# One bank for both heads of a pair in the attention units with one or two blocks of keys, and eight low parts of the output weights on POOL

## The chip, the cores and the metric

The kernel runs on one core of a Trainium2 chip. The metric is the device time of one execution in microseconds (us). The engines are named as in the profile: PE is TensorE, with PEld its weight loads; DVE is VectorE, ACT ScalarE, POOL GpSimd, SP SyncE. SP issues most of the DMAs.

## The reference

Two layers; each is a feed-forward block, a token mixer and a second feed-forward block, each followed by a layer norm. The sequence has 512 positions, the model 1024 features. The change lies in the mixer, whose attention parts are these, per block of 128 queries:

```
def diff_attention_block(q_blk, start, k1, k2, v, lam):     # 4 heads, two softmaxes each
    def probs(qi, ki):
        sc = jnp.einsum('bhqd,bhkd->bhqk', qi, ki).astype(jnp.float32) * scale
        return jax.nn.softmax(jnp.where(causal, sc, -jnp.inf), axis=-1)
    w = probs(q1, k1) - lam * probs(q2, k2)
    return jnp.einsum('bhqk,bhkd->bhqd', w.astype(v.dtype), v)

def stick_breaking_block(q_blk, start, k, v):                # 4 heads
    z = jnp.einsum('bhqd,bhkd->bhqk', q_blk, k).astype(jnp.float32) * (B_HEAD_DIM ** -0.5)
    log_stay = jnp.where(strict, jax.nn.log_sigmoid(-z), 0.0)
    log_tail = lax.cumsum(log_stay, axis=3, reverse=True) - log_stay
    w = jnp.where(strict, jnp.exp(jax.nn.log_sigmoid(z) + log_tail), 0.0)
    return jnp.einsum('bhqk,bhkd->bhqd', w.astype(v.dtype), v)
```

The third part of the mixer is a gated delta rule over chunks, which needs the inverses of triangular matrices and then a scan over the sequence. The three outputs are normed, the third is gated, and the concatenation is multiplied with the output weights (1024 by 1024).

## The kernel before

All data are 32-bit and feature-major. A product with weights is three matmuls (L103 to L105): the activations and the weights are each split into a high part and a low part, and the product of the two low parts is left out. Weights come from HBM in chunks of 512 KB (L81) to a ring of two buffers. ACT casts each half of a chunk to the high part (L89); the low part is the difference (L90), on DVE or, where `st.eng` says so, on POOL. In the mixer, from the first projections on, `st.eng` is POOL, until `st.eng = st.queue = None` ahead of the output projection. Such a weight tile has 24 matmuls of 512 columns, called fills below where they go into time that other work leaves on PE.

The order of the instructions on each engine comes from a scheduler that goes by dependencies, buffers and the order in which the program emits its work, so a change in the emission moves rows on every engine. In the mixer the emission is this: query and key projections of the stick-breaking heads; values; `attend(1, 0)` and `attend(1, 1)` (stick-breaking, a pair of heads each); twelve convolved tiles; one projection of queries and keys for the differential heads; `triangles()`; `attend(0, 0)`, in which `between` emits the second such projection (its evictions are L510 on ACT and L511 on DVE); `delta()`; `attend(0, 1)`; `outputs()`; the four gate tiles; the output projection with its norm.

- `attend` works on a pair of heads in units, one for a block of 128 queries (qt 0 to 3) and one head: (qt 2, 3, 1, 0) by two heads, eight units. A unit of block qt has (qt + 1) blocks of keys. The `between` work is emitted after the fourth unit. Each unit's values are emitted one unit later (`later`).
- `unit` takes a score bank in PSUM for each score row (`psc`, two banks), L880 and L881. For the differential heads there are two score rows each: maximum (L917), exponential with its sum (L467), then a reciprocal (L922), a factor (L923) and the combination (L926). For stick-breaking heads: absolute value (L933), exponential and logarithm (L467 twice), L936, a scan from the back (L939), L940, an exponential (L467). The values are transposes to the bank `pt` (L904), a copy (L906) and the products to the bank `po` (L909).
- `triangles` ends in `base`: blocks of 16 by 16 go to the scratch in HBM (L675) and back in another layout (L692), are inverted on DVE in fifteen pairs of dependent operations (L700, L702), copied (L704), written out (L703, L705) and read back as `XT` and `X` (L708, L710). The names in the profile of what is read are `XT` and `inv`.
- `delta` doubles the inverted blocks: for each of four heads products L718, L723 and transposes L727, with an ACT copy or a DVE subtraction (L724) after each. `join` (L738 to L752) follows.
- `outputs` is the scan over the chunks (`scan`, L773 to L798), in which a product waits for DVE and DVE for a product; the norms of its results (`emit`).
- The output projection (`head`) first multiplies the first half of the contraction for four output tiles, which takes eight parts of weights (a part is half a chunk), then the other half, and adds each tile to the norm's sums (L157 to L168).

Of the kernel before, what the change touches and what calls it, by code (L numbers as in the profile page):

```python
# [9 lines left out]
F32 = mybir.dt.float32  # L10
# [416 lines left out]
def mixer(g, l):  # L427
# [446 lines left out]
    def scores(q, k, qt, i, which):  # L874

        n = (qt + 1) * P
        dgn = ch(qt)
        sc = py()
        for j, t in enumerate(k[i]):
            nc.tensor.matmul(out=sc[:, 0:n], lhsT=q[i][0][:, dgn], rhs=t[:, 0:n], start=j == 0, stop=False)  # L880
        nc.tensor.matmul(out=sc[:, dgn], lhsT=g.identb, rhs=g.maskb[:, which], start=False, stop=True)  # L881
        return sc

    def attend(which, j, between=None):
# [3 lines left out]
        units = [(qt, i) for qt in (2, 3, 1, 0) for i in range(2)]  # L888
        for n, (qt, i) in enumerate(units):
            nxt = unit(which, qt, 2 * j + i, po, su[:, qt, i], P * qt + 64 * i)  # L890
            while len(later) > 1:
                later.pop(0)()
            later.append(nxt)
            if between and n == 3:
                between()
        later.append(lambda: finish(which, j, po, su))

    def unit(which, qt, h, po, su, col):
        n = (qt + 1) * P

        def values(w):
            pt = pav.tile([P, T], F32, name="pt")
            for k in range(qt + 1):
                nc.tensor.transpose(out=pt[:, ch(k)], in_=w[:, ch(k)], identity=g.ident)  # L904
            wT = at.tile([P, T], F32, name="at")
            nc.scalar.copy(out=wT[:, 0:n], in_=pt[:, 0:n])  # L906
            vc = 256 * which + 64 * h
            for k in range(qt + 1):
                nc.tensor.matmul(out=po[:, col:col + 64], lhsT=wT[:, ch(k)], rhs=V[k][:, vc:vc + 64],  # L909
                                 start=k == 0, stop=k == qt)  # L910

        def diff():
            mx = sm.tile([P, 2], F32, name="mx")
            pr = []
            for i in range(2):
                sc = scores(qa, ka, qt, 2 * h + i, 0)
                nc.vector.tensor_reduce(out=mx[:, i:i + 1], in_=sc[:, 0:n], axis=mybir.AxisListType.X, op=ALU.max, negate=True)  # L917
                p = at.tile([P, T], F32, name="at")
                act(out=p[:, 0:n], in_=sc[:, 0:n], func=AF.Exp, bias=mx[:, i:i + 1], accum_out=su[:, i:i + 1])
                pr.append(p)  # L920
            cf = sm.tile([P, 2], F32, name="cf")
            nc.vector.reciprocal(out=cf[:, 0:1], in_=su[:, 1:2])  # L922
            nc.vector.scalar_tensor_tensor(out=cf[:, 1:2], in0=su[:, 0:1], scalar=g.nlam[:, l:l + 1], in1=cf[:, 0:1],  # L923
                                           op0=ALU.mult, op1=ALU.mult)
            p1, p2 = pr
            nc.vector.scalar_tensor_tensor(out=p1[:, 0:n], in0=p2[:, 0:n], scalar=cf[:, 1:2], in1=p1[:, 0:n],  # L926
                                           op0=ALU.mult, op1=ALU.add)
            return lambda: values(p1)

        def stick():  # L930
            sc = scores(qb, kb_, qt, h, 1)
            e = at.tile([P, T], F32, name="at")
            nc.scalar.activation(out=e[:, 0:n], in_=sc[:, 0:n], func=AF.Abs)  # L933
            act(out=e[:, 0:n], in_=e[:, 0:n], func=AF.Exp, scale=-1.0)
            act(out=e[:, 0:n], in_=e[:, 0:n], func=AF.Ln, bias=1.0)
            nc.vector.scalar_tensor_tensor(out=e[:, 0:n], in0=sc[:, 0:n], scalar=0.0, in1=e[:, 0:n], op0=ALU.max, op1=ALU.add)  # L936
            cs = e
            back = e[:, 0:n][:, ::-1]
            nc.vector.tensor_tensor_scan(out=cs[:, 0:n][:, ::-1], data0=back, data1=back, initial=0.0, op0=ALU.add, op1=ALU.bypass)  # L939
# [319 lines left out]
```

## Time and profile before

| | |
|---|---|
| median of three runs | 2250.42 us (2246.45 to 2251.85) |
| profiled execution, its own time | 2250.16 us |
| its span, first to last instruction | 2248.4 us |
| mean granted clock of TensorE in it | 0.985 of full |
| PE busy | 2138.2 us, 95% of the span |
| DVE, ACT, POOL busy | 1169.6, 907.9 and 377.5 us |

The profile is of one execution. Busy PE time is modelled for pipelined matmuls, so that one matmul's duration overlaps the next one's. The times of a row are from the start of the span. The first layer's mixer runs from about 400 to 760 us, the second layer's from about 1515 to 1875 us, with the same pattern.

### The profile page before, as it was taken

The numbers are of one execution on the slowest core, as the hardware profiler recorded it, in microseconds if no ns is written. First come the engines' busy times: TensorE is split into PE (matmuls) and PEld (weight loads), VectorE is DVE, ScalarE is ACT, GpSimd is POOL, SyncE is SP. The second block draws the span as 40 slices with busy tenths as digits, with TensorE's granted clock in tenths as the row PEclk, the third lists the DMA queues.
The fourth block names the chain that finished last, engine by engine and source line by source line (L and its number), as shares of the span: only waits on it lengthen the run. The fifth ranks groups of instructions, "written<-read, shape, count | busy, mean of one in ns | idle before, by whom it ended". The sixth has DMA issues, their size and how long they took to land. (4 is left out here: it accounts for less than half of the span.)

```text
span 2248.4 us, 30132 instructions
## 1 busy us (share of the span) xinstructions
PE 2138.2 (95%) x11382; PEld 1782.6 (79%) x11382; DVE 1169.6 (52%) x2363; ACT 907.9 (40%) x1801; POOL 377.5 (17%) x327
## 2 busy tenths in 40 slices
PE   8999999999798999999999999999987989999997
PEld 7888889777677888888888888897776768888886
DVE  4533436386578833343663334263774788333426
ACT  4333324575464533332443333245753535333313
POOL 1100011426204400000130000023461234000010
PEclk9999999999899999999999999999998999999998
DMA  6423323514512233332333333234144123333322
GB/s 190 125 94 95 98 75 104 139 40 122 129 58 72 84 109 94 94 94 75 116 109 95 94 94 94 66 104 131 57 133 109 48 85 94 95 96 100 95 66 94
DMA packets 90898, 217.32 MB, mean 97 GB/s; under 512 B 21968, under 2 KB 36336, under 8 KB 90752
## 3 DMA queue, kind: packets, MB, share of 16 engines
q1 hardware_dynamic: 82848, 187.47, 27.5%
q10 hardware_dynamic: 6912, 25.17, 3.8%
q0 software_dynamic: 992, 2.75, 0.7%
q8 instruction: 90, 1.47, 0.3%
q14 instruction: 56, 0.46, 0.1%
HBM read 193.83 MB, written 6.83 MB: 89 GB/s over the span
## 5 line engine op out<-in xcount | busy, mean ns | idle before, releaser
L89 ACT CAST whi<-wraw 128x512 fp32r<-128x512 f32 x692 | 421.4, 619 | 959.4 <-PE pd L104 755.1
L90 DVE TENSOR_TENSOR wlo<-wraw,whi 128x512 fp32r<-128x512 f32 x580 | 431.0, 751 | 658.6 <-ACT whi L89 647.4
L103 PE MATMUL pd<-x,whi 128*128 128x512 f32 (+1 forms) x1920 | 726.7, 380 | 12.9 <-ACT x L1177 6.2
L105 PE MATMUL pd<-x,wlo 128*128 128x512 f32 (+1 forms) x1920 | 728.3, 380 | 3.2 <-DVE wlo L90 3.2
L104 PE MATMUL pd<-x,whi 128*128 128x512 f32 (+1 forms) x1920 | 727.7, 379 | 1.6 <-POOL x L231 1.3
L103 PEld LDWEIGHTS pd<-x,whi 128*128 128x128 f32 x1920 | 365.8, 191 | 77.5 <-ACT x L1177 6.2
L105 PEld LDWEIGHTS pd<-x,wlo 128*128 128x128 f32 x1920 | 366.2, 191 | 67.4 <-DVE wlo L90 3.4
L104 PEld LDWEIGHTS pd<-x,whi 128*128 128x128 f32 x1920 | 366.2, 191 | 66.8 <-POOL x L231 3.0
L103 PE MATMUL pd<-hhi,whi 128*128 128x512 f32 (+1 forms) x880 | 307.7, 350 | 0.0
L104 PE MATMUL pd<-hlo,whi 128*128 128x512 f32 (+1 forms) x880 | 307.7, 350 | 0.0
L105 PE MATMUL pd<-hhi,wlo 128*128 128x512 f32 (+1 forms) x880 | 307.3, 349 | 0.0
L168 POOL TENSOR_TENSOR lt<-lt 128x512 f32<-128x512 f32 x26 | 38.9, 1497 | 1065.3 <-ACT lt L165 1065.3
L103 PEld LDWEIGHTS pd<-hhi,whi 128*128 128x128 f32 x880 | 165.5, 188 | 24.4
L105 PEld LDWEIGHTS pd<-hhi,wlo 128*128 128x128 f32 x880 | 165.4, 188 | 24.1
L104 PEld LDWEIGHTS pd<-hlo,whi 128*128 128x128 f32 x880 | 165.5, 188 | 24.1
L90 POOL TENSOR_TENSOR wlo<-wraw,whi 128x512 fp32r<-128x512 f32 x112 | 150.2, 1357 | 138.7 <-ACT whi L89 70.1
L259 DVE TENSOR_TENSOR lt<-pd,lt 128x512 f32<-128x512 f32 x88 | 60.4, 689 | 111.9 <-PE pd L105 110.7
L231 POOL TENSOR_TENSOR x<-x 128x256 fp32r<-128x256 f32 x60 | 45.1, 753 | 162.5 <-ACT x L229 132.7
L134 POOL TENSOR_TENSOR x<-x 128x512 f32<-128x512 f32 x48 | 70.9, 1522 | 0.0
L261 DVE TENSOR_TENSOR hlo<-lt,hhi 128x512 fp32r<-128x512 f32 x88 | 67.0, 765 | 6.3
L165 ACT ACTIVATE lt<-x 128x256 f32<-128x256 f32 (+1 forms) x58 | 29.7, 512 | 95.8 <-DVE x L163 95.5
L568 DVE SCALAR_TENSOR_TENSOR kqv<-pd,conv,kqv 128x511 f32<-128x511 f32 (+2 forms) x72 | 53.5, 743 | 20.1 <-ACT kqv L566 18.9
(309 smaller groups left out, 2287.9 us busy)
## 6 DMA issues: line engine op xcount, KB each, us to landing
wraw<-in_w SPq DMA_DIRECT2D x308, 512.0 KB, 3.5
wraw<-in_w ACTq DMA_DIRECT2D x48, 512.0 KB, 3.6
kqv<-kqv SPq DMA_DIRECT2D x128, 64.0 KB, 2.0
kqv<-kqv SPq DMA_DIRECT2D x48, 128.0 KB, 4.7
scr<-zero POOLq DMA_DIRECT2D x2, 1032.0 KB, 11.1
x<-in_xT SPq DMA_DIRECT2D x8, 256.0 KB, 5.5
scr<-inv SPq DMA_DIRECT2D x8, 256.0 KB, 2.7
XT<-scr SPq DMA_DIRECT2D x8, 256.0 KB, 4.8
```

Of the source, the lines that this page charges most:

```text
L89: nc.scalar.copy(out=hi, in_=r)
L90: (eng or self.eng or nc.vector).tensor_tensor(out=lo, in0=r, in1=hi.bitcast(F32), op=ALU.subtract)
L103: nc.tensor.matmul(out=out, lhsT=whi, rhs=xhi, start=first, stop=False)
L104: nc.tensor.matmul(out=out, lhsT=whi, rhs=xlo, start=False, stop=False)
L105: nc.tensor.matmul(out=out, lhsT=wlo, rhs=xhi, start=False, stop=last)
L134: i = g.nc.gpsimd.tensor_tensor(out=t, in0=xhi.bitcast(F32), in1=xlo.bitcast(F32), op=ALU.add)
L165: nc.scalar.activation(out=sq[:, r], in_=t[:, r], func=AF.Square)
L168: eng.tensor_tensor(out=self.acc2[:, r], in0=self.acc2[:, r], in1=sq[:, r], op=ALU.add)
L231: eng.tensor_tensor(out=xlo[:, r], in0=t[:, r], in1=xhi[:, r].bitcast(F32), op=ALU.subtract)
L259: nc.vector.tensor_tensor(out=sg, in0=pu, in1=sg, op=ALU.mult)
L261: nc.vector.tensor_tensor(out=hlo, in0=sg, in1=hhi.bitcast(F32), op=ALU.subtract)
L568: nc.vector.scalar_tensor_tensor(out=y[:, s:], in0=p[:, :T - s], scalar=wc[:, 3 - s:4 - s], in1=y[:, s:], op0=ALU.mult, op1=ALU.add)
```

## The change

A unit with one or two blocks of keys now takes both heads of the pair. The score rows of both heads stand side by side in one bank of 512 columns: for stick-breaking heads two rows of 256 or 128 columns, for differential heads two rows of 256 to a bank (two banks) or four rows of 128. Operations without a scalar of their own per row go over the whole bank: the maximum (now L928, with two or four results), the reciprocal and the factor (L936, L937), the stick-breaking chain except its scan, and the copy of the transposed weights. The exponentials of the differential heads, the scans and the combinations (now L941) stay one per row or head. `attend` so has six units for eight. The `between` work is emitted after the third unit. In the output projection `st.eng` stays POOL for the first half's eight parts of weights.

```diff
-    def scores(q, k, qt, i, which):
-
-        n = (qt + 1) * P
+    def scores(out, q, k, qt, i, which):
+
         dgn = ch(qt)
-        sc = py()
         for j, t in enumerate(k[i]):
-            nc.tensor.matmul(out=sc[:, 0:n], lhsT=q[i][0][:, dgn], rhs=t[:, 0:n], start=j == 0, stop=False)
-        nc.tensor.matmul(out=sc[:, dgn], lhsT=g.identb, rhs=g.maskb[:, which], start=False, stop=True)
-        return sc
+            nc.tensor.matmul(out=out, lhsT=q[i][0][:, dgn], rhs=t[:, 0:(qt + 1) * P], start=j == 0, stop=False)
...
-        units = [(qt, i) for qt in (2, 3, 1, 0) for i in range(2)]
-        for n, (qt, i) in enumerate(units):
-            nxt = unit(which, qt, 2 * j + i, po, su[:, qt, i], P * qt + 64 * i)
+        units = [(2, (0,)), (2, (1,)), (3, (0,)), (3, (1,)), (1, (0, 1)), (0, (0, 1))]
+        for n, (qt, hs) in enumerate(units):
+            nxt = unit(which, qt, j, hs, po, su)
             while len(later) > 1:
                 later.pop(0)()
             later.append(nxt)
-            if between and n == 3:
+            if between and n == 2:
                 between()
...
-    def unit(which, qt, h, po, su, col):
+    def unit(which, qt, j, hs, po, su):
         n = (qt + 1) * P
-
-        def values(w):
+        m = len(hs)
+        heads = [2 * j + i for i in hs]
+
+        def values(ws):
             pt = pav.tile([P, T], F32, name="pt")
-            for k in range(qt + 1):
-                nc.tensor.transpose(out=pt[:, ch(k)], in_=w[:, ch(k)], identity=g.ident)
+            for i, w in enumerate(ws):
+                for k in range(qt + 1):
+                    nc.tensor.transpose(out=pt[:, i * n + k * P:i * n + (k + 1) * P], in_=w[:, ch(k)], identity=g.ident)
             wT = at.tile([P, T], F32, name="at")
-            nc.scalar.copy(out=wT[:, 0:n], in_=pt[:, 0:n])
-            vc = 256 * which + 64 * h
-            for k in range(qt + 1):
-                nc.tensor.matmul(out=po[:, col:col + 64], lhsT=wT[:, ch(k)], rhs=V[k][:, vc:vc + 64],
-                                 start=k == 0, stop=k == qt)
+            nc.scalar.copy(out=wT[:, 0:m * n], in_=pt[:, 0:m * n])
+            for i, h in enumerate(heads):
+                vc = 256 * which + 64 * h
+                col = P * qt + 64 * hs[i]
+                for k in range(qt + 1):
+                    nc.tensor.matmul(out=po[:, col:col + 64], lhsT=wT[:, i * n + k * P:i * n + (k + 1) * P],
+                                     rhs=V[k][:, vc:vc + 64], start=k == 0, stop=k == qt)
...
+        def parts(x, c):
+            return [x[:, i * n:(i + 1) * n] for i in range(c)]
 
         def diff():
-            mx = sm.tile([P, 2], F32, name="mx")
+            mx = sm.tile([P, 4], F32, name="mx")
+            todo = [(h, i) for h in range(m) for i in range(2)]
+            per = T // n
             pr = []
-            for i in range(2):
-                sc = scores(qa, ka, qt, 2 * h + i, 0)
-                nc.vector.tensor_reduce(out=mx[:, i:i + 1], in_=sc[:, 0:n], axis=mybir.AxisListType.X, op=ALU.max, negate=True)
+            for a in range(0, 2 * m, per):
+                now = todo[a:a + per]
+                c = len(now)
+                sc = py()
+                for (h, i), o in zip(now, parts(sc, c)):
+                    scores(o, qa, ka, qt, 2 * heads[h] + i, 0)
+                nc.vector.tensor_reduce(out=mx[:, a:a + c], in_=sc[:, 0:c * n].rearrange("p (c t) -> p c t", t=n),
+                                        axis=mybir.AxisListType.X, op=ALU.max, negate=True)
                 p = at.tile([P, T], F32, name="at")
-                act(out=p[:, 0:n], in_=sc[:, 0:n], func=AF.Exp, bias=mx[:, i:i + 1], accum_out=su[:, i:i + 1])
-                pr.append(p)
-            cf = sm.tile([P, 2], F32, name="cf")
-            nc.vector.reciprocal(out=cf[:, 0:1], in_=su[:, 1:2])
-            nc.vector.scalar_tensor_tensor(out=cf[:, 1:2], in0=su[:, 0:1], scalar=g.nlam[:, l:l + 1], in1=cf[:, 0:1],
+                for b, ((h, i), o, y) in enumerate(zip(now, parts(sc, c), parts(p, c))):
+                    act(out=y, in_=o, func=AF.Exp, bias=mx[:, a + b:a + b + 1], accum_out=su[:, qt, hs[h], i:i + 1])
+                    pr.append(y)
+            cf = sm.tile([P, 2, 2], F32, name="cf")
+            sv = su[:, qt, hs[0]:hs[0] + m]
+            nc.vector.reciprocal(out=cf[:, 0:m, 0], in_=sv[:, :, 1])
+            nc.vector.scalar_tensor_tensor(out=cf[:, 0:m, 1], in0=sv[:, :, 0], scalar=g.nlam[:, l:l + 1], in1=cf[:, 0:m, 0],
...
-            p1, p2 = pr
-            nc.vector.scalar_tensor_tensor(out=p1[:, 0:n], in0=p2[:, 0:n], scalar=cf[:, 1:2], in1=p1[:, 0:n],
-                                           op0=ALU.mult, op1=ALU.add)
-            return lambda: values(p1)
+            for h in range(m):
+                p1, p2 = pr[2 * h:2 * h + 2]
+                nc.vector.scalar_tensor_tensor(out=p1, in0=p2, scalar=cf[:, h, 1:2], in1=p1, op0=ALU.mult, op1=ALU.add)
+            return lambda: values(pr[::2])
...
-            sc = scores(qb, kb_, qt, h, 1)
+            sc = py()
+            for h, o in zip(heads, parts(sc, m)):
+                scores(o, qb, kb_, qt, h, 1)
+            sc = sc[:, 0:m * n]
             e = at.tile([P, T], F32, name="at")
-            nc.scalar.activation(out=e[:, 0:n], in_=sc[:, 0:n], func=AF.Abs)
-            act(out=e[:, 0:n], in_=e[:, 0:n], func=AF.Exp, scale=-1.0)
-            act(out=e[:, 0:n], in_=e[:, 0:n], func=AF.Ln, bias=1.0)
-            nc.vector.scalar_tensor_tensor(out=e[:, 0:n], in0=sc[:, 0:n], scalar=0.0, in1=e[:, 0:n], op0=ALU.max, op1=ALU.add)
-            cs = e
-            back = e[:, 0:n][:, ::-1]
-            nc.vector.tensor_tensor_scan(out=cs[:, 0:n][:, ::-1], data0=back, data1=back, initial=0.0, op0=ALU.add, op1=ALU.bypass)
-            nc.vector.tensor_tensor(out=cs[:, 0:n], in0=sc[:, 0:n], in1=cs[:, 0:n], op=ALU.subtract)
-            act(out=cs[:, 0:n], in_=cs[:, 0:n], func=AF.Exp)
-            return lambda: values(cs)
+            cs = e[:, 0:m * n]
+            nc.scalar.activation(out=cs, in_=sc, func=AF.Abs)
+            act(out=cs, in_=cs, func=AF.Exp, scale=-1.0)
+            act(out=cs, in_=cs, func=AF.Ln, bias=1.0)
+            nc.vector.scalar_tensor_tensor(out=cs, in0=sc, scalar=0.0, in1=cs, op0=ALU.max, op1=ALU.add)
+            for y in parts(e, m):
+                back = y[:, ::-1]
+                nc.vector.tensor_tensor_scan(out=back, data0=back, data1=back, initial=0.0, op0=ALU.add, op1=ALU.bypass)
+            nc.vector.tensor_tensor(out=cs, in0=sc, in1=cs, op=ALU.subtract)
+            act(out=cs, in_=cs, func=AF.Exp)
+            return lambda: values(parts(e, m))
...
-    st.eng = st.queue = None
+    st.queue = None
...
             if b < KD:
                 for d in range(4):
                     st.get(bo + d * KD + PC)
+                st.eng = None
                 st.use([g.ws] * 3 + [g.wx] * 5)
```

The built program has the same PE instructions in another order. On ACT it has 48 fewer of about 1790 over both layers, on DVE 68 fewer, 16 of them low parts (L90), which POOL has more. The order of three places follows, as rows of line, operation, output from inputs and shape.

On DVE, the beginning of the fifteen pairs of `base` in the first layer, while `attend(0, 0)` runs, before:

```order
L700 TENSOR_TENSOR blkt<-blk 128x15
L926 SCALAR_TENSOR_TENSOR at<-at,cf 128x512
L702 TENSOR_TENSOR blk<-blk,blkt 128x15
L917 TENSOR_REDUCE mx<-psc 128x1
L700 TENSOR_TENSOR blkt<-blk 128x28
L922 RECIPROCAL cf<-su 128x1
L917 TENSOR_REDUCE mx<-psc 128x1
L702 TENSOR_TENSOR blk<-blk,blkt 128x14x2
L923 SCALAR_TENSOR_TENSOR cf<-su,nlam,cf 128x1
L700 TENSOR_TENSOR blkt<-blk 128x39
L926 SCALAR_TENSOR_TENSOR at<-at,cf 128x512
L702 TENSOR_TENSOR blk<-blk,blkt 128x13x3
```

and of the change:

```order
L700 TENSOR_TENSOR blkt<-blk 128x15
L928 TENSOR_REDUCE mx<-psc 128x1
L702 TENSOR_TENSOR blk<-blk,blkt 128x15
L928 TENSOR_REDUCE mx<-psc 128x2
L700 TENSOR_TENSOR blkt<-blk 128x28
...
L928 TENSOR_REDUCE mx<-psc 128x2
L700 TENSOR_TENSOR blkt<-blk 128x48
L702 TENSOR_TENSOR blk<-blk,blkt 128x12x4
L700 TENSOR_TENSOR blkt<-blk 128x55
L702 TENSOR_TENSOR blk<-blk,blkt 128x11x5
L928 TENSOR_REDUCE mx<-psc 128x4
L700 TENSOR_TENSOR blkt<-blk 128x60
```

Before, reductions of one score row stand between the pairs; the eight of the one- and two-block units reach to the eleventh pair. In the change the reductions of those units are three, the last ahead of the sixth pair; from the first L700 to L704 it is 46 rows, where it was 55. The L511 that follows L704 (the second projection's keys) keeps its place.

On PE, from the last unit of `attend(0, 0)` to the doubling of the first heads, before (L103 to L105 are gate fills, L718, L723 and L727 the doubling):

```order
L909 MATMUL po<-kqv,at 128x64 x2
L904 MATMUL pt<-ident,at 128x128
L103 MATMUL pd<-x,whi 128x512
L104 MATMUL pd<-x,whi 128x512
L105 MATMUL pd<-x,wlo 128x512
...
L718 MATMUL pa<-inv,lt 128x128 x4
L105 MATMUL pd<-x,wlo 128x512
...
L723 MATMUL pa<-XT,inv 128x128 x4
L105 MATMUL pd<-x,wlo 128x512
...
L727 MATMUL pa<-ident,XT 128x128 x4
L718 MATMUL pa<-inv,lt 128x128 x4
```

and of the change:

```order
L911 MATMUL po<-kqv,at 128x64 x4
L904 MATMUL pt<-ident,at 128x128 x4
L103 MATMUL pd<-x,whi 128x512
L104 MATMUL pd<-x,whi 128x512
L105 MATMUL pd<-x,wlo 128x512
...
L105 MATMUL pd<-x,wlo 128x512
L718 MATMUL pa<-inv,lt 128x128 x4
L723 MATMUL pa<-XT,inv 128x128 x4
L727 MATMUL pa<-ident,XT 128x128 x4
L718 MATMUL pa<-inv,lt 128x128 x4
L723 MATMUL pa<-XT,inv 128x128 x4
```

Before, eight of the second gate tile's fills stood between the last L904 and the first L718, and its other sixteen behind it, among the first two heads. In the change the first gate tile's 24 fills stand ahead of the last scores, all 24 of the second's between the last L904 and the first L718, and none among the heads' L718, L723 and L727. Within the scan of `outputs`, from its first L779 to its last L798, stand 52 weight matmuls, where 35 stood.

On POOL, from the end of `triangles` to the first norm's application in the first layer (L995, now L1013, is the split of the attention outputs, L134 the residual, L168 a norm sum), before:

```order
L715 TENSOR_TENSOR lt<-inv,mask 128x512 x2
L695 MEMSET blk 128x256
L696 MEMSET blk 128x16
L90 TENSOR_TENSOR wlo<-wraw,whi 128x512 x2
L995 TENSOR_TENSOR kqv<-x,kqv 128x256 x8
L134 TENSOR_TENSOR x<-x 128x512 x8
L168 TENSOR_TENSOR lt<-lt 128x512 x3
L90 TENSOR_TENSOR wlo<-wraw,whi 128x512 x8
L231 TENSOR_TENSOR x<-x 128x256 x12
```

and of the change:

```order
L715 TENSOR_TENSOR lt<-inv,mask 128x512 x2
L90 TENSOR_TENSOR wlo<-wraw,whi 128x512
L695 MEMSET blk 128x256
L696 MEMSET blk 128x16
L90 TENSOR_TENSOR wlo<-wraw,whi 128x512 x7
L1013 TENSOR_TENSOR kqv<-x,kqv 128x256 x8
L134 TENSOR_TENSOR x<-x 128x512 x8
L90 TENSOR_TENSOR wlo<-wraw,whi 128x512 x2
L168 TENSOR_TENSOR lt<-lt 128x512 x2
L90 TENSOR_TENSOR wlo<-wraw,whi 128x512
L168 TENSOR_TENSOR lt<-lt 128x512
L90 TENSOR_TENSOR wlo<-wraw,whi 128x512 x7
L231 TENSOR_TENSOR x<-x 128x256 x12
```

Six of the eight moved low parts stand ahead of the split of the attention outputs; two stand behind the residual, and the third norm sum stands behind one low part that is loaded ahead.

## Rows read from the trace of the kernel before

**Rows 1.** The page, busy time, share of the span and count of each engine.

```profile
PE 2138.2 (95%) x11382; PEld 1782.6 (79%) x11382; DVE 1169.6 (52%) x2363; ACT 907.9 (40%) x1801; POOL 377.5 (17%) x327
```

**Rows 2.** Stretches: length, busy us of PE, PEld, DVE, ACT, POOL, granted clock, DMA.

```profile
430.00:512.00 82.00, 77.63 (x412) 60.27 (x411) 62.63 (x122) 59.20 (x138) 28.02 (x21) 0.98 0.15 45
571.00:581.00 10.00, 7.82 (x27) 5.81 (x27) 7.61 (x19) 4.52 (x12) 4.58 (x6) 0.50 0.53 116
576.00:602.00 26.00, 19.74 (x103) 15.90 (x102) 15.02 (x62) 9.06 (x28) 2.55 (x2) 0.83 0.33 73
620.00:660.00 40.00, 40.00 (x402) 31.14 (x402) 28.42 (x83) 22.89 (x65) 0.00 (x0) 1.00 0.18 54
660.00:700.00 40.00, 34.40 (x209) 27.26 (x208) 29.84 (x112) 18.95 (x46) 15.96 (x16) 1.00 0.05 14
723.00:730.00 7.00, 1.44 (x9) 1.22 (x8) 6.93 (x14) 2.68 (x6) 4.05 (x4) 0.86 0.33 88
1690.00:1716.00 26.00, 18.31 (x105) 15.06 (x105) 15.15 (x62) 9.08 (x29) 2.55 (x2) 0.89 0.36 78
```

**Rows 3.** ACT by line and shape, 430 to 760: busy us, mean ns, idle before.

```profile
L467 ACT ACTIVATE at<-at 128x256 f32<-128x256 f32 x12 | 4.7, 411 | 0.2
L467 ACT ACTIVATE at<-at 128x128 f32<-128x128 f32 x12 | 3.7, 306 | 1.6 <-DVE at L940 1.6
```

**Rows 4.** DVE and POOL by line and shape in the same stretch.

```profile
L917 DVE TENSOR_REDUCE mx<-psc 128x1 f32<-128x512 f32 x8 | 5.4, 680 | 1.1 <-PE psc L881 1.1
L917 DVE TENSOR_REDUCE mx<-psc 128x1 f32<-128x256 f32 x8 | 3.3, 416 | 3.2 <-PE psc L881 3.2
L917 DVE TENSOR_REDUCE mx<-psc 128x1 f32<-128x128 f32 x8 | 2.3, 289 | 1.1 <-PE psc L881 1.0
L922 DVE RECIPROCAL cf<-su 128x1 f32<-128x1 f32 x16 | 2.5, 157 | 1.4 <-ACT at L467 1.4
L923 DVE SCALAR_TENSOR_TENSOR cf<-su,nlam,cf 128x1 f32<-128x1 f32 x16 | 4.5, 283 | 0.1
L90 DVE TENSOR_TENSOR wlo<-wraw,whi 128x512 fp32r<-128x512 f32 x19 | 14.3, 770 | 11.1 <-ACT whi L89 11.1
L90 POOL TENSOR_TENSOR wlo<-wraw,whi 128x512 fp32r<-128x512 f32 x43 | 58.5, 1376 | 56.7 <-ACT whi L89 24.2 <-ACT at L467 10.4 <-PE pd L104 7.0
```

**Rows 5.** DVE in order of time around base: start, us, work, wait before it.

```profile
578.40 0.18 DVE L702 TENSOR_TENSOR blk<-blk,blkt 128x15 f32<-128x15 f32 x1
580.96 0.42 DVE L917 TENSOR_REDUCE mx<-psc 128x1 f32<-128x256 f32 x1 [2.39 <-PE psc L881]
592.70 1.12 DVE L702 TENSOR_TENSOR blk<-blk,blkt 128x15 f32<-128x15 f32 x1
593.86 0.37 DVE L704 COPY blk<-blk 128x256 f32<-128x256 f32 x1
594.15 0.68 DVE L511 SCALAR_TENSOR_TENSOR kqv<-pd,kqv 128x512 fp32r<-128x512 f32 x1
```

**Rows 6.** POOL in order of time beside them.

```profile
592.53 1.26 POOL L90 TENSOR_TENSOR wlo<-wraw,whi 128x512 fp32r<-128x512 f32 x1 [5.23 <-ACT whi L89]
```

**Rows 7.** PE in order of time from base to the doubling.

```profile
594.89 0.79 PE L103 MATMUL pd<-x,whi 128*128 128x512 f32 x1 [2.35 <-DVE kqv L511]
595.48 0.63 PE L104 MATMUL pd<-x,whi 128*128 128x512 f32 x1
595.90 0.63 PE L105 MATMUL pd<-x,wlo 128*128 128x512 f32 x1
601.92 2.04 PE L718 MATMUL pa<-inv,lt 128*128 128x128 f32 x8 [3.36 <-DMA inv<-scr]
608.87 1.06 PE L718 MATMUL pa<-inv,lt 128*128 128x128 f32 x8
613.04 1.06 PE L718 MATMUL pa<-inv,lt 128*128 128x128 f32 x8
617.26 1.06 PE L718 MATMUL pa<-inv,lt 128*128 128x128 f32 x8
```

More of the change, by code (lines that the diff above doesn't have):

```diff
@@ L872, in mixer @@
     oab = [None] * 4
-    def scores(q, k, qt, i, which):
-        n = (qt + 1) * P
+    def scores(out, q, k, qt, i, which):
         dgn = ch(qt)
-        sc = py()
         for j, t in enumerate(k[i]):
-            nc.tensor.matmul(out=sc[:, 0:n], lhsT=q[i][0][:, dgn], rhs=t[:, 0:n], start=j == 0, stop=False)
-        nc.tensor.matmul(out=sc[:, dgn], lhsT=g.identb, rhs=g.maskb[:, which], start=False, stop=True)
-        return sc
+            nc.tensor.matmul(out=out, lhsT=q[i][0][:, dgn], rhs=t[:, 0:(qt + 1) * P], start=j == 0, stop=False)
+        nc.tensor.matmul(out=out[:, dgn], lhsT=g.identb, rhs=g.maskb[:, which], start=False, stop=True)
     def attend(which, j, between=None):
```

## The prediction

> **What bounds the kernel now.** I read the page's busy times first: PE is busy 95% of the span, the next engine 52% [rows 1]. So nothing is gained by less work on ACT or DVE as such, only where PE waits for them. The table of stretches then says where that is. In the stick-breaking stretch of 82 us PE works 77.63 and sits idle 4.37, with ACT busy 59.20 and DVE 62.63. Around `base` it works 19.74 of 26 us at a granted clock of 0.83; in the second layer's like stretch 18.31 of 26 at 0.89. For the ten us from 571 the clock is 0.50, its lower level of 1.2 GHz. From 620 to 660 PE has no idle time at all, from 660 to 700, in the scan, 5.60 us; and in the output projection it works 1.44 of the 7 us from 723, with DVE busy 6.93 [rows 2]. Last I read DVE and PE in order of time around `base`. There one chain sets the end: the fifteen pairs on DVE finish at L704 (593.86), the inverse goes to HBM and back, and the first product that uses it starts at 601.92, 8.06 us later, after PE has waited 3.36 [rows 5, 7]. Ahead of that PE waited 2.35 for an L511 that stands behind L704 on DVE, because its bank had to come free for a gate fill [rows 5, 7].
>
> **The change part by part.** All for one layer; the second is taken alike, by the two stretches above.
>
> *Stick-breaking units.* Of the sixteen units, eight become four. Each shared one drops three activations, an absolute value and a copy on ACT, and two operations on DVE. An activation of 256 columns takes 0.411 us and two of 128 take 0.612 [rows 3], so about 0.20 goes with each of 20 ACT operations: 4.0 us of 59.20. I price the eight dropped DVE operations like the reductions, 2 x 0.289 - 0.416 = 0.16 each [rows 4]: 1.3 us of 62.63. Neither engine sets the pace; PE's idle time of 4.37 is the most there is to gain. Against it, a shared unit gives its first head's weights out only when both are done. The shared operations are about 0.1 longer each (0.411 against 0.306) [rows 3], and the second head's scan comes on top; at half a us for each of four units that nothing covers, the loss is 2. Between -4.4 and +2 I take -1.0, nearer to none, since all 77.63 us of PE's work stay.
>
> *`attend(0, 0)`, `base` and the doubling.* On DVE a pair of heads loses these: four maxima of 256 columns become two of 512 (4 x 0.416 - 2 x 0.680 = 0.30), four of 128 one of 512 (4 x 0.289 - 0.680 = 0.48), and two reciprocals with their factors go (2 x (0.157 + 0.283) = 0.88): 1.66 us [rows 4]. From the first pair's L702 (578.40) to L704 are 15.46 us. In them the pairs stood behind reductions that waited for scores, 2.39 us the longest, and one L702 of 15 columns took 1.12 instead of 0.18, while POOL ran a low part [rows 5, 6]. In the built order the two-block scores stand together on PE and no reduction stands behind the sixth pair, so later pairs can't wait for scores. Of the 1.66 only the 0.88 lies in this stretch (its three maxima of 512 for 4 x 0.416 and 4 x 0.289 cost within 0.8 of the same, as a maximum of a three-block pair's last row moves in). I add 1.1, about half the longest wait, and let L704 be 2.0 earlier. It can be none, or a loss of 2.4, if the four one-block rows bring one more such wait ahead of the sixth pair; at best 2.0 + 2.39/2 + 0.94 = 4.1.
>
> The 8.06 us from L704 to the first product are DMA steps that stay. What PE does in them changes: 24 gate fills for 8. The fills are behind L511 as before. At the lower clock they follow each other by 0.42 us (595.48, 595.90) [rows 7]; eight at that and sixteen at half of it take 3.4 + 3.4 = 6.8, within 8.06. With none left in the doubling, its first head should go at the pace of the unfilled ones, 617.26 - 613.04 = 4.22, where it took 608.87 - 601.92 = 6.95 [rows 7]: 2.7 less. Nothing behind absorbs that, as PE is full from 620 to 660. Together -4.7; but with its fills issued earlier PE now stands idle from the attention's end to L511, some 5.5 us for 2.35 (15 fills of 0.21 that stood among the one-block scores come earlier), and idle time there was followed by the lower clock: the first L718 group took 2.04, behind a wait of 3.36, and the later ones 1.06 [rows 7]. Two such groups more at the lower clock (2 x 0.98), or the fills wholly at it (24 x 0.42 = 10.1, 2.0 past 8.06), take 2.0 back. So -2.7, between -6.8 and +4.4 (L704 2.4 later and the 2.0).
>
> *Second differential pair, the scan, low parts.* `attend(0, 1)` loses the same 1.66 us of DVE work, and the six moved low parts 6 x 0.770 = 4.6 [rows 4], beside a full PE. The scan now holds 52 weight matmuls for 35, out of the stretch in which PE is full. 17 at 0.21 are 3.6 us, which the scan's idle 5.60 can take in [rows 2, 7]. But each may stand ahead of a product that the recurrence waits for, and POOL's low parts (1.376 each) run beside DVE. From -5.6 (all idle gone) to +3.6 (the fills only lengthen the scan) I take -1.8, half of the fills.
>
> *Output projection.* The other two low parts leave DVE before the stretch with the 5.56 us of PE idle time (7 - 1.44) [rows 2], 1.5 us less work; against it the third norm sum stands on POOL behind a low part of 1.376 [rows 4]. These cancel: 0, between -1.5 and +1.4.
>
> The sum is -1.0 - 2.7 - 1.8 + 0 = -5.5 a layer, -11 for both. The profiled execution took 2250.16, which gives 2239.2; the runs' median is 0.3 above it, so I say 2239.5.
>
> In that sum DVE and POOL work side by side: the L702 of 1.12 us lay beside POOL's low part of 1.26 at 592.53, where the same shape took 0.18 at 578.40 [rows 5, 6]. The Trainium skill, GPSIMD Engine Reference, section "Key points", says the same against the change: POOL shares its SBUF interfaces with VectorE, and the two contend where a DVE operation has two SBUF inputs. The trace agrees, with 1.12 against 0.18; by that rule each moved part can cost a DVE operation as much, which is the small gain below.
>
> **The rivals.**
> *No change, 2249 (chance 0.23).* What goes on ACT and DVE was hidden anyway. For it: PE's 95%, and only 4.37 us of idle in the stick-breaking stretch. Then its term is 0, L704 stays, since the four-row maximum brings a wait like the 2.39 lost, and the scan stays set by its recurrence. What is left is the doubling's 2.7 less the 2.0: -0.7 a layer, 2248.8.
>
> *A small gain, 2247 (0.08).* Each of the eight low parts on POOL stretches one DVE operation by 1.12 - 0.18 = 0.94, four of them on the scan's path: +3.8 of 5.5, leaves -1.7 a layer, 2246.8. Against it: six of the eight stand ahead of the scan's end beside a full PE.
>
> *Slower, 2259 (0.15).* One mechanism, at `base`: the fills that kept PE busy during `attend(0, 0)`'s end are spent early, PE idles from the last values to L511 and stays at 0.50 through fills and doubling. The fills run 2.0 past the read-back, and each head's two groups of eight (L718, L723) and its transposes cost 2.04 - 1.06 = 0.98, 0.98 and half of it more, 2.45 for a head, of which the unfilled pace of 4.22 hides none: 9.8 for four. With the 2.0, less the doubling's 2.7, the scan's 1.8, the stick-breaking 1.0 and L704's 2.0, this is +4.3 a layer, 2258.8. It decides if the clock is still low at the second head. For it: the ten us at 0.50 from 571 [rows 2]. Against: after its wait of 3.36 PE was at the lower clock for the first L718 group only, 2.04 and then 1.06 [rows 7].
>
> *A larger gain, 2227 (0.14).* The ten us at 0.50 from 571, with 7.82 us of work, shrink to half, as the merged scores come with fewer breaks: 2.0 more; half of the stick-breaking idle goes (1.2 more), and no clock loss at the doubling (2.0 more), 0.6 in the scan: -11.3 a layer, 2227.6.
>
> **How the numbers follow.** The forecast's own case has 0.40, with 2232 to 2246. 0.3%, what a measurement of this kernel can tell from none, is 6.75 us: faster is below 2243.7, slower above 2257.2. Faster: 0.40 x 0.9, the larger gain 0.14, and a little of the small gain, 0.53 in all. Slower: 0.15, and 0.02 of the no-change case. Same: 0.30. The range from 2226 to 2257 takes in all but part of the slower case and the tail of the larger.
>
> **What would show it.** Right: L704 some 2 us earlier after the first L700; 24 fills in one block between L511 and the first L718; first heads 4.2 apart; less idle PE time in the scan; both layers alike. Wrong: a DVE wait for scores ahead of the sixth pair as long as 2.39; a granted clock of 0.50 through the doubling; more PE idle time from 430 to 512; L702, or the scan's operations, at about 1.1 us beside POOL.

## The result: 1.3% slower, and the profile after

The changed kernel took 2275.40 us, median of six runs (2273.53 to 2281.03), against 2247.34 (2245.12 to 2251.85) of the kernel before; the ratio is 1.0127, interval 1.011 to 1.0144. A time of 2239.5 was forecast. The profiled execution has a span of 2274.6 us, 26.2 more than before, with less to do on ACT and DVE. First the page's busy times, as in [rows 1]:

```profile
PE 2144.6 (94%) x11382; PEld 1790.1 (79%) x11382; DVE 1185.4 (52%) x2295; ACT 902.6 (40%) x1753; POOL 402.4 (18%) x343
```

DVE has 68 instructions fewer and is busy 15.8 us longer. That is the first sign: some of its operations have become longer. Next the stretches that answer to [rows 2]: stick-breaking, a part of the convolutions, `base` (26 us up to the first L718), the scan from its first L779 to its last L798, and the output projection's wait:

```profile
430.00:512.00 82.00, 74.47 (x402) 58.95 (x403) 60.18 (x110) 56.42 (x118) 27.72 (x21) 0.98 0.14 45
515.00:525.00 10.00, 7.08 (x28) 5.59 (x27) 5.08 (x7) 6.07 (x12) 7.71 (x6) 0.80 0.44 128
584.00:610.00 26.00, 22.02 (x97) 18.21 (x97) 16.33 (x55) 9.40 (x31) 4.71 (x6) 0.67 0.50 114
659.78:704.58 44.80, 36.06 (x217) 29.64 (x216) 32.43 (x85) 14.37 (x33) 18.34 (x18) 0.89 0.07 24
740.00:747.00 7.00, 1.25 (x7) 1.22 (x7) 6.93 (x14) 2.68 (x6) 4.04 (x3) 0.70 0.34 92
```

PE sits idle 7.53 us in the stick-breaking stretch, where it was 4.37, and 8.74 in the scan. The scan of before, cut in the same way, is shorter:

```profile
652.84:689.34 36.50, 32.75 (x232) 27.89 (x232) 26.57 (x99) 19.43 (x50) 15.96 (x16) 1.00 0.06 20
```

Where the first layer's time went is read best from a few marks in the order of time: what starts when, in both traces.

| mark, first layer | before | after | later by | of it in this step |
|---|---|---|---|---|
| first L673 (`triangles`) | 559.14 | 568.10 | 9.0 | 9.0 |
| L704 (end of the fifteen pairs) | 593.86 | 601.52 | 7.7 | -1.3 |
| first L718 | 601.92 | 609.87 | 8.0 | 0.3 |
| first L738 (end of doubling) | 621.57 | 627.07 | 5.5 | -2.5 |
| first L779 (scan) | 652.84 | 659.78 | 6.9 | 1.4 |
| end of the last L798 | 689.34 | 704.58 | 15.2 | 8.3 |
| L179 of the output projection | 728.87 | 745.76 | 16.9 | 1.7 |

So two steps lost 9.0 and 8.3 us, and `base` and doubling gained 3.5. Of the 9.0, 1.5 were there before the first attention unit's work on ACT began: its absolute value (L933, now L951) starts at 434.60 for 433.13. From there to the first L673, the stick-breaking and conv stretch, it is this, before and after, the second layer behind the first:

```profile
433.13:559.14 126.01, 119.36 (x622) 95.81 (x621) 93.61 (x178) 84.27 (x187) 58.51 (x44) 0.99 0.25 73
1548.14:1673.26 125.12, 117.48 (x621) 94.42 (x621) 93.54 (x178) 84.22 (x187) 58.49 (x44) 1.00 0.24 74
```

```profile
434.60:568.10 133.50, 120.66 (x621) 98.47 (x620) 92.79 (x170) 82.80 (x167) 59.38 (x44) 0.96 0.24 70
1559.92:1692.48 132.56, 119.42 (x621) 97.82 (x620) 93.08 (x170) 82.78 (x167) 59.41 (x44) 0.97 0.24 71
```

The stretch loses 7.5 us in the first layer and 7.4 in the second, most of it as idle time of PE (12.84 for 6.65 in the first). The scan has 44.8 us again in the second layer (1786.13 to 1830.97). From its first L951 to its L179 the second layer loses 14.3 us. Between the two mixers, from the first layer's L179 to that L951, where the change edits nothing, this execution took 814.16 us for 819.27; so the span is 26.2 us longer and not twice 16.9. PE in order of time shows the waits of the change, in the stick-breaking and conv stretch, at the doubling and in the scan, with what ended each:

```profile
476.32 0.47 PE L103 MATMUL pd<-x,whi 128*128 128x512 f32 x1 [1.80 <-DVE kqv L568]
499.85 0.63 PE L990 MATMUL pt<-ident,at 128*128 128x128 f32 x4 [3.54 <-DVE at L984]
521.80 1.11 PE L581 MATMUL pa<-ident,kqv 128*128 128x128 f32 x4 [2.92 <-POOL kqv L576]
602.55 0.80 PE L103 MATMUL pd<-x,whi 128*128 128x512 f32 x1 [1.35 <-DVE kqv L511]
609.87 1.05 PE L718 MATMUL pa<-inv,lt 128*128 128x128 f32 x8
614.03 1.06 PE L718 MATMUL pa<-inv,lt 128*128 128x128 f32 x8
618.20 1.06 PE L718 MATMUL pa<-inv,lt 128*128 128x128 f32 x8
682.21 1.22 PE L773 MATMUL pa<-S,kqv 128*128 128x128 f32 x4 [4.34 <-DVE S L792]
687.74 0.77 PE L779 MATMUL pa<-inv,XT 128*128 128x128 f32 x2 [2.60 <-DVE inv L775]
```

Each long wait ends with DVE or POOL. Before, the transposes of the same pair (then L972) waited 0.72:

```profile
503.85 0.66 PE L972 MATMUL pt<-ident,at 128*128 128x128 f32 x4 [0.72 <-DVE at L966]
```

What DVE did ahead of the L984 for which the transposes L990 waited is the norm of the second stick-breaking pair, small operations of eight columns:

```profile
493.82 1.22 DVE L111 TENSOR_SCALAR af<-ams 128x8 int32<-128x8 int32 x1
495.07 1.21 DVE L114 TENSOR_TENSOR arr_t<-af 128x8 f32<-128x8 f32 x1
496.32 1.18 DVE L115 SCALAR_TENSOR_TENSOR arr_t<-arr_t,ams 128x8 f32<-128x8 f32 x1
497.54 0.17 DVE L116 SCALAR_TENSOR_TENSOR af<-arr_t,af 128x8 f32<-128x8 f32 x1
```

and POOL beside it:

```profile
493.71 2.55 POOL L90 TENSOR_TENSOR wlo<-wraw,whi 128x512 fp32r<-128x512 f32 x2
496.22 1.27 POOL L576 TENSOR_TENSOR kqv<-kqv,lt 128x512 f32<-128x512 f32 x1
```

Three POOL operations, three DVE operations of 1.2 us; once POOL is done (497.49) the next takes 0.17. At 0.17 each these three would have ended 3.1 us earlier, of the 3.54 that PE waited. In the scan DVE does the same for the norms of its results, in one queue with the operations that the recurrence waits for:

```profile
677.04 1.20 DVE L114 TENSOR_TENSOR orr_t<-of 128x4 f32<-128x4 f32 x1
678.27 1.18 DVE L115 SCALAR_TENSOR_TENSOR orr_t<-orr_t,oms 128x4 f32<-128x4 f32 x1
679.49 1.18 DVE L116 SCALAR_TENSOR_TENSOR of<-orr_t,of 128x4 f32<-128x4 f32 x1
680.60 0.33 DVE L792 SCALAR_TENSOR_TENSOR S<-S,eG,pa 128x128 f32<-128x128 f32 x1
685.62 1.71 DVE L819 TENSOR_TENSOR o<-o,of 128x512 f32<-128x512 f32 x1
```

and on POOL at that time are the residual adds:

```profile
676.95 9.83 POOL L134 TENSOR_TENSOR x<-x 128x512 f32<-128x512 f32 x8
```

The L792, which reads a bank of PSUM and one tile of SBUF, keeps its 0.33 in the middle of it. It comes late because it stands behind the others. Before, the residual adds ran from 678.43, when the second chain of norms was at its last operation, L819:

```profile
677.84 1.19 DVE L819 TENSOR_TENSOR o<-o,of 128x512 f32<-128x512 f32 x1
678.43 10.38 POOL L134 TENSOR_TENSOR x<-x 128x512 f32<-128x512 f32 x8
```

In the change the attention is through earlier against the scan, so its splits and then the residual adds start earlier against it, 17.2 us after the scan's start for 25.6. Added up from 400 to 1880 us, DVE operations that took over 0.15 us more than the short ones of their form (the shortest tenth) have 110 us too many after and 88 before, and every one of them overlaps a POOL operation. The sum alone decides nothing, though: the fastest version below has 95. What counts is which operations are held, and whether PE waits behind them.

Two lines of [rows 5] have these answers. The wait ahead of the sixth pair is there, but 1.23 where 2.39 went:

```profile
595.17 0.69 DVE L928 TENSOR_REDUCE mx<-psc 128x4 f32<-128x512 f32 x1 [1.23 <-PE psc L879]
601.52 0.37 DVE L704 COPY blk<-blk 128x256 f32<-128x256 f32 x1
```

### The profile page after: what moved, and what is told of

Same layout as the page of the kernel before. It is cut to its first block, busy times and chain, and to the rows that moved or that the text cites. A ratio compares the mean times of both kernels' runs of the same rounds, so it can differ in the third digit from the quotient of the medians.

```text
span 2274.6 us, 30014 instructions
## 1 busy us (share of the span) xinstructions
PE 2144.6 (94%) x11382; PEld 1790.1 (79%) x11382; DVE 1185.4 (52%) x2295; ACT 902.6 (40%) x1753; POOL 402.4 (18%) x343
## 4 chain that ended last, share of the span: by engine, by line
PE 56%; DVE 15%; ACT 4%; DMA 3%; issue 2%; POOL 1%; ACTq 0%; POOLq 0%; DVEq 0%; SPq 0%
PE pd L104 16%; PE pd L103 16%; PE pd L105 16%; DMA wraw<-in_w 3%; DVE wlo L90 2%; ACT whi L89 1%; PE po L911 1%; DVE at L957 1%; POOL wlo L90 1%; PE psc L878 1%; DVE kqv L568 1%; DVE lt L166 1%; ACT at L467 1%; DVE x L212 1%; DVE x L220 1%
## 5 line engine op out<-in xcount | busy, mean ns | idle before, releaser
L90 DVE TENSOR_TENSOR wlo<-wraw,whi 128x512 fp32r<-128x512 f32 x564 | 422.9, 758 | 637.7 <-ACT whi L89 629.3
L103 PE MATMUL pd<-x,whi 128*128 128x512 f32 (+1 forms) x1920 | 728.5, 381 | 16.7 <-ACT x L1196 6.6
L105 PE MATMUL pd<-x,wlo 128*128 128x512 f32 (+1 forms) x1920 | 725.5, 378 | 2.6 <-DVE wlo L90 2.6
L103 PEld LDWEIGHTS pd<-x,whi 128*128 128x128 f32 x1920 | 365.5, 191 | 83.7 <-ACT x L1196 6.9
L105 PEld LDWEIGHTS pd<-x,wlo 128*128 128x128 f32 x1920 | 366.3, 191 | 67.4 <-DVE wlo L90 2.8
L103 PE MATMUL pd<-hhi,whi 128*128 128x512 f32 (+1 forms) x880 | 307.7, 350 | 0.0
L105 PE MATMUL pd<-hhi,wlo 128*128 128x512 f32 (+1 forms) x880 | 307.2, 349 | 0.0
L90 POOL TENSOR_TENSOR wlo<-wraw,whi 128x512 fp32r<-128x512 f32 x128 | 171.8, 1353 | 319.0 <-ACT whi L89 260.6
L168 POOL TENSOR_TENSOR lt<-lt 128x512 f32<-128x512 f32 x26 | 41.1, 1579 | 1035.3 <-ACT lt L165 1035.1
L103 PEld LDWEIGHTS pd<-hhi,whi 128*128 128x128 f32 x880 | 165.4, 188 | 24.4
L105 PEld LDWEIGHTS pd<-hhi,wlo 128*128 128x128 f32 x880 | 165.4, 188 | 24.2
L568 DVE SCALAR_TENSOR_TENSOR kqv<-pd,conv,kqv 128x511 f32<-128x511 f32 (+2 forms) x72 | 53.6, 745 | 36.1 <-ACT kqv L566 34.7
L134 POOL TENSOR_TENSOR x<-x 128x512 f32<-128x512 f32 x48 | 70.2, 1507 | 0.0
```

The source lines that it names most:

```text
L90: (eng or self.eng or nc.vector).tensor_tensor(out=lo, in0=r, in1=hi.bitcast(F32), op=ALU.subtract)
L103: nc.tensor.matmul(out=out, lhsT=whi, rhs=xhi, start=first, stop=False)
L105: nc.tensor.matmul(out=out, lhsT=wlo, rhs=xhi, start=False, stop=last)
L134: i = g.nc.gpsimd.tensor_tensor(out=t, in0=xhi.bitcast(F32), in1=xlo.bitcast(F32), op=ALU.add)
L168: eng.tensor_tensor(out=self.acc2[:, r], in0=self.acc2[:, r], in1=sq[:, r], op=ALU.add)
L568: nc.vector.scalar_tensor_tensor(out=y[:, s:], in0=p[:, :T - s], scalar=wc[:, 3 - s:4 - s], in1=y[:, s:], op0=ALU.mult, op1=ALU.add)
```

## The experiments

The ratio of each is to the kernel before, timed beside it on the same chip. The theory: the loss is DVE operations held beside POOL, in the scan by splits and residual adds, in the conv stretch by weight parts and products; the low parts themselves matter little. Rivals: the eight low parts on POOL do it; the weight matmuls in the scan do it; the shared units make the path longer by themselves.

**The parts of the change alone.** Low parts taken back:

```diff
-    st.queue = None
+    st.eng = st.queue = None
...
-                st.eng = None
```

> The change with the eight low parts of output weights back on DVE. Theory (the merged units let POOL's later work, the splits L1013 and residual adds L134, fall on the norm chains of the scan, and the shared stick-breaking units bring POOL work and waits into the conv stretch): the loss stays, 2266 to 2277. Rival (the eight low parts on POOL are what DVE collides with): back to 2240 to 2252.

2277.36, ratio 1.0121 (1.0102 to 1.0141): the loss stays. Scan 45.8 us. Then the opposite, only these two lines in the kernel before:

> The kernel before with only the eight low parts moved to POOL. Theory: within 2244 to 2253. Rival (low parts on POOL): 2263 to 2276.

2272.01, ratio 1.0096 (1.008 to 1.0112). Here the theory missed: alone, the low parts cost three quarters of what all three cost together. Its trace has the scan at 41.89 us, with L134 from 677.50 on beside the chains: the order shifts with the moved parts, and the collision in the scan comes by another way. That is 5.4 us a layer; another 6.3 in the first layer and 3.5 in the second came between the first L673 and the scan, and their cause stays open. Next the units, shared for one kind alone, with the low parts as before:

```diff
+        if which == 0:      # 1 in the second run
+            units = [(qt, (i,)) for qt in (2, 3, 1, 0) for i in range(2)]
...
-            if between and n == 2:
+            if between and n == len(units) // 2 - 1:
```

> The kernel before with shared units for stick-breaking heads alone; differential units and low parts as before. Theory: the stick-breaking and conv stretch loses some 9 us a layer and the scan nothing, 2260 to 2267. Rival: 2244 to 2251.

> The kernel before with shared units for differential heads alone (with the second projection after the third of six units); stick-breaking units and low parts as before. Theory: base and doubling gain 3 to 4 us a layer, the scan loses about 8, 2252 to 2260. Rival: the predicted gain without loss, 2238 to 2244.

2265.45 (1.0067, 1.005 to 1.0084) and 2264.66 (1.0067, 1.0048 to 1.0085). With stick-breaking units alone the same waits stand in the conv stretch (3.52 for L992, 2.90 for L581) and the scan is 38.6 us. With differential ones alone there is no such wait, L738 is 3.9 us earlier than before, and the scan is 45.15. Each loses in the place that the theory names; the second is 5 us above its range.

**The residual adds held.** A semaphore's wait, until the scan's last norm is done; PE's and DVE's order in the scan stays:

```diff
-        nm.residual(d)
+        nm.residual(d, normed[-1], True)
```

> The change with one wait more: the eight residual adds (L134 on POOL) start only when the last norm of the scan (L819, now L837) is done; the order on PE, DVE and ACT stays but for a few rows behind the scan. Theory (L134 beside the norm chains stretches DVE operations with two SBUF inputs, and the scan waits behind them): first L779 to last L798 falls from 44.8 us to 36 to 39, the time to 2258 to 2266. Rival (the scan is longer because 52 weight matmuls stand in it for 35): 44 to 46, 2272 to 2279.

2269.82, ratio 1.0098 (1.0081 to 1.0115). The scan came to 35.11 us for 44.80, with the same 52 weight matmuls in it:

```profile
656.75:691.86 35.11, 32.94 (x217) 27.15 (x216) 24.43 (x85) 14.34 (x33) 8.55 (x10) 1.00 0.10 31
```

The rival of the fills falls. PE's idle time in the scan went from 8.74 us to 2.17, and its same 217 matmuls took 3.1 us less, at a granted clock of 1.00 for 0.89. The same DVE operations as above, now without POOL, and what came later:

```profile
674.00 0.16 DVE L114 TENSOR_TENSOR orr_t<-of 128x4 f32<-128x4 f32 x1
674.20 0.16 DVE L115 SCALAR_TENSOR_TENSOR orr_t<-orr_t,oms 128x4 f32<-128x4 f32 x1
674.39 0.16 DVE L116 SCALAR_TENSOR_TENSOR of<-orr_t,of 128x4 f32<-128x4 f32 x1
674.47 0.34 DVE L792 SCALAR_TENSOR_TENSOR S<-S,eG,pa 128x128 f32<-128x128 f32 x1
675.64 0.69 DVE L819 TENSOR_TENSOR o<-o,of 128x512 f32<-128x512 f32 x1
703.11 5.70 DVE L1013 TENSOR_TENSOR kqv<-x,kqv 128x256 fp32r<-128x256 f32 x4
```

The time fell less than the scan, and lies 4 us above the theory's range, since the held adds now lie on the splits of the scan's own outputs (four L1013 in 5.70 us, 0.42 each without POOL), for which PE waits:

```profile
706.05 0.79 PE L104 MATMUL pd<-kqv,whi 128*128 128x512 f32 x1 [3.01 <-DVE kqv L1013]
```

Also the splits of the attention outputs on DVE (`split(o)` for `split(o, nc.gpsimd)`):

> As the run before, and the splits of the attention outputs (L1013) on DVE for POOL, so that in the scan POOL has only weight parts. Theory: another 1 to 2 us a layer off the scan, 2254 to 2264. Rival (fills): 2272 to 2279, as 3.3 us of work come to DVE and nothing leaves the path.

2269.08, ratio 1.0091 (1.0075 to 1.0108): no difference that can be told, and 5 above the theory's range. The scan's 33.4 us are 1.7 less; why the time doesn't show them stays open. The same wait in the kernel before, with the order on PE, DVE, ACT and POOL unchanged:

> The kernel before with the same wait ahead of the residual adds as in the first run of this set; the order is that of before on every engine. Theory: the scan's 3.0 us of stretched DVE time there go in part, the output projection starts no later, 2243 to 2250. Rival (fills): 2247 to 2254, no gain and the residual later.

2263.54, ratio 1.0067 (1.0048 to 1.0086), against both expectations: the scan stays 36.5, as its first chains had been clear of L134 already, and the 3.01 and 1.17 us of waits for L995 come in.

**The chains taken away.** The attention norms' inverse square root on ACT, which runs logarithms and exponentials in the mixer in any case (L467):

```diff
-        rsqrt(g, sm, f, ms, 8, "arr")
+        act(out=f, in_=ms, func=AF.Ln)
+        act(out=f, in_=f, func=AF.Exp, scale=-0.5)
```

> The change with the inverse square root of the attention norms (ten small DVE operations for each of four pairs of heads) as logarithm and exponential on ACT; it is a little less exact. Theory (POOL stretches the chain of the second stick-breaking pair, behind which the transposes L990 stand on PE): their wait of 3.5 us goes, and with it the lower clock behind it, 3 to 5 us a layer, 2264 to 2270. Rival (the wait comes from the place of L990 in the order, or from ACT): 2272 to 2279.

2260.37, ratio 1.0051 (1.0034 to 1.0068). That is 4 us below the theory's range. The stick-breaking and conv stretch takes 126.93 us in the first layer and 127.29 in the second: 6.6 of the 7.5 and 5.3 of the 7.4 are gone, though ten operations of 0.17 were only 1.7 us of work. The edit also moved some other rows of the stretch, on PE and POOL too, and no run holds POOL off this chain alone, so POOL's part in the loss is read from the rows above and not tested by itself. L990 (now L991) still waits, for less:

```profile
491.07 0.66 PE L991 MATMUL pt<-ident,at 128*128 128x128 f32 x4 [1.96 <-DVE at L985]
```

The scan, whose norms are untouched, stays at 43.4:

```profile
650.60:694.00 43.40, 32.70 (x198) 27.26 (x198) 31.12 (x75) 14.66 (x34) 18.35 (x18) 0.92 0.08 25
```

The same edit in the kernel before:

> The kernel before with the attention norms' inverse square root alone on ACT, the same edit as the run of the change that came to 2260. Theory: the stick-breaking and conv stretch keeps its length within 2 us of before, since there the chain lay clear of most POOL work; the time hangs on where the scan's chains then meet POOL, 2240 to 2262. Rival (the edit itself is worth 8 us a layer): 2228 to 2236.

2268.96, ratio 1.0085 (1.007 to 1.01), 7 above the range. The conv stretch kept its length (first L673 at 558.59), but L134 came to run from 675.86, and the scan is 41.7 us. The scan's loss is about half of the whole. And both kinds of norms on ACT, in the change and in the kernel before; the second edit is the first's in `emit`:

```diff
-        rsqrt(g, sm, ff, msf, 2 * n, "orr")
+        act(out=ff, in_=msf, func=AF.Ln)
+        act(out=ff, in_=ff, func=AF.Exp, scale=-0.5)
```

> The change with the inverse square roots of the attention norms and of the scan's norms as logarithm and exponential on ACT, so that beside POOL's splits and residual adds DVE has few operations with two SBUF inputs left (a little less exact). Theory (these chains beside POOL are the loss): first L779 to last L798 35 to 38 us, 2236 to 2250. Rival (merged units lengthen the path of attention and scan by themselves): 2255 or more.

> The kernel before with both inverse square roots on ACT as in the run above. Theory: a little faster than before, 2236 to 2248, and with the chains out of POOL's way the merged units of the run above are 0 to 11 us faster than this. Rival: the run above stays 8 us or more slower than this one.

2232.16, ratio 0.993 (0.9915 to 0.9944), the fastest version of all and 4 below the theory's range, and 2247.45, ratio 0.999 (0.998 to 0.9999). The scans, in this order:

```profile
650.07:681.19 31.12, 29.91 (x198) 25.10 (x198) 19.32 (x51) 12.43 (x35) 18.87 (x18) 1.00 0.11 34
```

```profile
658.85:690.05 31.20, 29.26 (x192) 23.66 (x192) 21.43 (x54) 13.36 (x36) 16.62 (x16) 1.00 0.11 34
```

They are alike, POOL's work still beside them. The first has as many matmuls, 198, as the scan of 43.4 above: with the inverse roots of its norms off DVE it is 12.3 us shorter. And there the change is worth 15 us, above the 0 to 11 expected. L704 comes 3.4 us earlier in it, and from the first L718 to the first L738 it takes 17.2 us for 20.35. So the rival that the shared units lengthen the path falls too. The 15 us flatter the change, though. In the second kernel no gate fill stands between the attention's last products and the first L718, and PE waits 8.06 us there, where it was 3.36 before:

```profile
604.18 2.04 PE L718 MATMUL pa<-inv,lt 128*128 128x128 f32 x8 [8.06 <-DMA inv<-scr]
```

From the first L673 to the scan that kernel takes 100.3 us, where before took 93.7; the 5.3 us that its scan gained are lost there. Holding the residual adds on top, behind the last L1013:

> As the first run of this set, with the residual adds held until the last split of the scan's outputs on DVE (L1013) is done, so that they lie beside neither. Theory: within 6 us of the first run of this set, 2234 to 2250. Rival (residual adds late for the norm's sums): 5 to 15 us slower than it.

2247.60, ratio 0.999 (0.9981 to 1.0), 15.4 us behind the run without it and so the rival's side: they now lie beside the norm's sums, and PE waits 3.37 us for an L163 there.

**What each edit is worth then.** Norms on ACT throughout:

> The change with both kinds of inverse square roots on ACT (the run that came to 2232), but with the eight low parts of output weights back on DVE. Theory (the low parts cost only by moving the splits and residual adds against the norm chains): 2229 to 2238. Rival (they stretch DVE operations themselves): 2220 to 2228. If the low parts were a gain by themselves: 2239 to 2246.

> As the first run of this set (norms on ACT, low parts on DVE), with shared units for stick-breaking heads alone. By the prediction's terms (2 us for both layers of 11): 2243 to 2248, against 2247 without any shared unit. If the shared stick-breaking units carry the gain: 2232 to 2238.

> As the first run of this set, with shared units for differential heads alone (the second projection after the third of six units). By the prediction's terms (base, doubling and scan, 9 us for both layers): 2235 to 2241, against 2247 without any shared unit. If the stick-breaking units carry the gain: 2244 to 2249.

2235.95 (0.9935, 0.9913 to 0.9956), 2243.89 (0.9973, 0.9963 to 0.9983) and 2239.77 (0.9954, 0.9939 to 0.9968). All three lie in their ranges. Against 0.999 without any of it, the stick-breaking units are worth 0.0017 or 4 us (the two intervals overlap, so this is barely told from none), the differential ones 0.0036 or 8, both 0.0055 or 12; the low parts make no difference that can be told.

## Why the prediction was wrong, point by point

- *Stick-breaking units, -1.0, bounds to +2:* wrong, +7.5 and +7.4 in the two layers. I priced the longer hand-over of a shared unit. What came was a chain of small DVE operations beside POOL's weight parts, 3.54 us in one wait, and the lower clock behind it (a granted clock of 0.59 from 499.85 to 503.50, with 0.63 us for a weight matmul, and 0.39 after). With the chain on ACT 6.6 and 5.3 of it are gone. That the other waits there (2.92 for L581, 1.80 for L568) follow from it was not tested: the product L576 for which that L581 waited stood on POOL behind a weight part that ended at 520.52.
- *`base` and doubling, L704 2.0 earlier and -2.7 for the fills, less 2.0 for the clock:* right for the doubling, which gained 2.5 with the fills in one block and its heads 4.2 us apart, as forecast. L704 gained 1.3 by itself in the first layer and lost 0.7 in the second. PE waited 1.35 ahead of the fills, not 5.5, and the first L718 ran at the higher clock (1.05, where [rows 7] has 2.04), so the slower rival's mechanism did not come, though the clock up to there was 0.67 where it was 0.83.
- *The scan, -1.8:* wrong, +8.3, and this is the failed step. I counted fills and recurrence and let POOL's part end with the low parts. I had the measured collision in hand [rows 5, 6] and gave it a chance of 0.08, for the moved parts only, at one operation of 0.94 a part. The resident POOL work, eight splits and eight residual adds, was not asked where it would lie against the norms of the scan. One POOL operation after another held one small operation after another: from 677.04 to 687.25 DVE did eight of them, at 7.9 us more than the same operations took with the adds held. The prediction's own list had the sign, the scan's operations at about 1.1 us beside POOL, but no case of it carried more than the moved parts.
- *Output projection, 0:* +1.7 in the first layer, just outside its bounds, and -1.0 in the second; not tested.
- The size of the gain, with the sum of -11, is borne out where the chains are out of POOL's way: 12 to 15 us. The comparison is with a kernel whose order left PE waiting ahead of the first L718, so the agreement is in part luck.
- The forecast rested on before as a neutral ground. It was a favoured one: of the five kernels with a part of the change or all of it, norms on DVE and adds unheld, each lost at one of the two places or both, 0.7 to 1.3%; and so did before itself with only its attention norms on ACT (0.85%).

## What to carry to other kernels

Before pricing a change that shifts one stage against another, list what POOL runs in each and which DVE chains of small operations with SBUF inputs can come beside it, and price every link of such a chain at a whole POOL operation, not at its own length. If the order of a tuned kernel happens to keep the two apart, shorten or move the chain first, and only then judge the change. Holding POOL back with a wait moves the collision rather than ending it, if another DVE stage follows.

## What the runs showed of the hardware that was not expected

A DVE operation of four columns with two SBUF inputs, 0.16 us alone, takes up to 1.2 us beside POOL operations of 1.2 to 1.3, and a chain of them takes about one POOL operation each: the two engines step in turn. In these traces it also holds for a TENSOR_SCALAR with a single SBUF input (L111, 1.22 for 0.17), but not for a TENSOR_REDUCE of one SBUF tile (L971, 0.68 at 492.52, all of it beside POOL's L576), nor for operations that read PSUM and one SBUF tile (L792, 0.33; L781, 0.41).
